# A transformer block on one core: the order of its 512 and 256 column products

## The chip, the core and the metric

The kernel runs on one core of one Trainium2 chip. The metric is the device time of one execution in microseconds (us). Engines are named as in the profile: PE (TensorE matmuls), PEld (its weight loads), DVE (VectorE), ACT (ScalarE), POOL (GpSimd), SP (the DMA queue). L197 is line 197 of the kernel.

## The reference, cut to what matters

One layer of an encoder with 256 tokens, width 2048, float32:

```python
u = rmsnorm(h, g); z = u @ w_in               # 2048 -> [B|C|V|Q|K|V|gate_a|gate_b]
y_a = (b_a * dwconv3(c_a * v_a)) @ w_out_a    # 1024 -> 2048
y_b = windowed_attention(rope(q), rope(k), v, sink) @ w_o_attn
h = h + (sigmoid(gl_a + b) * y_a + sigmoid(gl_b + b) * y_b) @ w_mix_out
up = dwconv3(rmsnorm(h, g2) @ ffn_w_up) + bias          # 2048 -> 2 x 5632
h = h + (silu(up_a) * up_b) @ ffn_w_down                # 5632 -> 2048
return rmsnorm(h, g3)
```

## The kernel before

Nearly all time goes into seven matrix products, each with the 256 tokens as columns. A product is cut into **jobs**: one job makes 128 output rows by adding up `n` blocks of 128 x 128 weights in one PSUM bank (`ps`). `n` is 16 for the input projection, the mixing product and the up-projection, 8 for `w_out_a` and `w_o_attn`, 44 for the down-projection.

Float32 values are split in two: a high part, rounded to the format that PE reads at full rate, and a low part, the rest. The moving operand of a block lies as 512 columns, [high | low] of 256 tokens each (`xs`, `ya_att`, `ms`, `hs`, `actA`, `actC` through the stages). The weights come by DMA as `raw` in chunks of up to eight blocks; ACT makes their high part `whi` (L166), DVE the low part `wlo` (L177). For each block PE then issues two products, called a **pair** here: `whi` times all 512 columns (L197), and `wlo` times the 256 high columns (L198). The products of a job add up in its bank: columns 0 to 255 get high x high and low x high, columns 256 to 511 high x low; an eviction at the job's end adds both halves (`total`: ACT L226, DVE L230).

In a job's last block the order is turned: first the 256 column product, then the 512 column one (L202). The next job begins with its own 512 column product, so that at each job's end two 256s follow each other, and then two 512s. The very last job (`finale`) works with half of the tokens at a time and has an order of its own (L200).

Jobs follow each other in a written list, `groups`. A group of one job goes chunk by chunk of eight blocks. The first group, six jobs, runs block by block across all six; groups made by `outer_first` run three jobs (two in the down-projection) alternately in chunks of four blocks. What else an engine has to do is put between chunks by `run_due` and `step`: a function registered with `at(n, fn)` starts behind the n-th chunk, and a generator goes one step on behind each chunk. Attention's parts are placed so between chunks 29 and 75, and the second norm's sum over the squares (`inv_rms` called by `r2`: PE L240 into `nps`, then ACT, then DVE, a step behind each of three chunks) three chunks behind the end of the mixing product. DVE takes its work in program order, so that a `wlo` behind the norm's last step waits for it.

Of the kernel before, what the change touches and what calls it, by code (L numbers as in the profile page):

```python
# [16 lines left out]
T = 256  # L17
KT = D // P
# [33 lines left out]
def hybrid_block_kernel(ctx: ExitStack, tc: tile.TileContext, head, wide, xT, w_in, w_oa, w_o, w_mix, w_up, w_dn, vec, cst, out):  # L52
    nc = tc.nc
# [18 lines left out]
    def by_half(a):  # L72

        return a.rearrange("p (s h t) -> p h s t", s=2, h=2)
# [3 lines left out]
    def lazy(key, make):  # L78
        if key not in box:
            box[key] = make()  # L80
        return box[key]
# [3 lines left out]
    due, active = [], []  # L85
    now, count = [0], [0]

    def at(n, fn):
        due.append((n, count[0], fn))
        count[0] += 1  # L90
# [4 lines left out]
    def begin(fn, *args):  # L95
        g = fn(*args)
        if hasattr(g, "send") and next(g, 0) != 0:
            active.append(g)
# [6 lines left out]
    def finish():  # L105
        while active:
            step()

    def run_due():
        step()  # L110
        while True:
            ready = sorted(d for d in due if d[0] <= now[0])
            if not ready:
                return
            due.remove(ready[0])
            begin(ready[0][2])

    FETCH, HI, LO = 6, 3, 2
    bank_tags = {}

    def run(groups):

        chunks = []
        for size, jobs, wide in groups:
            n = jobs[0][1]
            if wide:  # L130
                for k in range(n):
                    chunks.append((None, [(job, k) for job in jobs], wide))
                continue
            for k0 in range(0, n, size):
                k1 = min(n, k0 + size)
                for job in jobs:
                    chunks.append((job[0][:, k0:k1, :], [(job, k) for k in range(k0, k1)], None))
        raws, his, los, banks = {}, {}, {}, {}

        def pieces(c):  # L140

            n = len(chunks[c][1])
            return ((0, 2), (2, n)) if c < 3 else ((0, n),)

        def fetch(c):
            w, blocks, pre = chunks[c]
            raw = wpool.tile([P, CH, P], F32, tag="raw", name="raw", bufs=5)
            if pre is not None:
                raws[c] = pre(0, c, raw)
            else:  # L150
                nc.sync.dma_start(raw[:, : len(blocks), :], w)
                raws[c] = lambda a, b, raw=raw: raw[:, a:b, :]


        def high(c):
            _, blocks, pre = chunks[c]
            if pre is not None:
                pre(1, c, None)
            (_, _, _, _, *halves), k0 = blocks[0]
            if halves:  # L160
                last = lazy("last", lambda: cpool.tile([P, FT, P], F32R, tag="B", name="last"))
                his[c] = last[:, k0 : k0 + len(blocks), :]
            else:
                his[c] = wpool.tile([P, CH, P], F32R, tag="whi", name="whi")
            for a, b in pieces(c):
                nc.scalar.copy(his[c][:, a:b, :], raws[c](a, b))  # L166
            if pre is not None:
                pre(2, c, None)

        def low(c):  # L170
            _, blocks, pre = chunks[c]
            if pre is not None:
                pre(3, c, None)
            los[c] = wpool.tile([P, CH, P], F32R, tag="wlo", name="wlo", bufs=3)
            raw = raws.pop(c)
            for a, b in pieces(c):
                nc.vector.tensor_tensor(los[c][:, a:b, :], raw(a, b), his[c][:, a:b, :], op=ALU.subtract)  # L177

        nxt = 0
        for c, (_, blocks, _) in enumerate(chunks):  # L180
            while nxt <= c + FETCH:
                for fn, i in ((fetch, nxt), (high, nxt - FETCH + HI), (low, nxt - FETCH + LO)):
                    if 0 <= i < len(chunks):
                        fn(i)
                nxt += 1
            hi, lo = his.pop(c), los.pop(c)
            ended = []
            for i, (job, k) in enumerate(blocks):
                _, n, rhs, epi, *halves = job
                if k == 0:  # L190
                    tag = bank_tags.get(id(job))
                    pool = aps if tag else lin
                    banks[id(job)] = pool.tile([P, 2 * T], F32, tag=tag or "ps", name="ps")
                ps = banks[id(job)]
                a, last = rhs(k), k == n - 1
                if not last and not (halves and k):
                    nc.tensor.matmul(ps, hi[:, i, :], a, start=k == 0, stop=False)  # L197
                nc.tensor.matmul(ps[:, 0:T], lo[:, i, :], a[:, 0:T], start=False, stop=False)  # L198
                if halves and k:
                    nc.tensor.matmul(by_half(ps)[:, 0], hi[:, i, :], by_half(a)[:, 0], start=False, stop=last)  # L200
                elif last:
                    nc.tensor.matmul(ps, hi[:, i, :], a, start=False, stop=True)  # L202
                if last:
                    ended.append(job)
            now[0] += 1
            run_due()
            for job in ended:
                begin(job[3], banks.pop(id(job)))
        finish()
# [25 lines left out]
    def inv_rms(parts, r, tag="tp"):  # L235

        n = r.shape[-1]
        acc = aps.tile([P, 2 * T], F32, tag=tag, name="nps")[:, 0:n]
        for i, a in enumerate(parts):
            nc.tensor.matmul(acc, ones, a, start=i == 0, stop=i == len(parts) - 1)  # L240
        yield 1
        r0 = spool.tile([P, T], F32, tag="sq", name="r0")[:, 0:n]
        nc.scalar.activation(r0, acc, AF.Ln, bias=eps)
        v = spool.tile([P, T], F32, tag="evt", name="nv")[:, 0:n]
        nc.vector.tensor_scalar(v, acc, EPS, None, op0=ALU.add)
        nc.scalar.activation(r0, r0, AF.Exp, scale=-0.5)
        yield 1

        t = spool.tile([P, T], F32, tag="evs", name="nt")[:, 0:n]
        nc.vector.tensor_tensor(t, r0, r0, op=ALU.mult)  # L250
        nc.vector.scalar_tensor_tensor(t, t, -0.5, v, op0=ALU.mult, op1=ALU.mult)
        nc.vector.scalar_tensor_tensor(r, t, 1.5, r0, op0=ALU.add, op1=ALU.mult)

    def new_r(name):
        rr["r"] = cpool.tile([P, T], F32, tag="r", name=name)
        return rr["r"]
# [190 lines left out]
    def att_turn(t, e):  # L447
        p = probs.pop((t, e))
        tp = aps.tile([P, 2, T], F32, tag="tp", name="ptp")
        for b in range(2):  # L450
            for n in range(2):
                nc.tensor.transpose(tp[:, b, n * P : (n + 1) * P], p[:, n, b * P : (b + 1) * P], ident)  # L452
        yield 1
        pT = p1.tile([P, 2, T], F32, tag="pT", name="pT", bufs=2)
        nc.scalar.copy(pT, tp)
        probs[t, e] = pT

    def att_out(t):
        kv = t // 4
        o = aps.tile([P, 2 * T], F32, tag="av", name="av")  # L460
        pT = [probs.pop((t, e)) for e in range(2)]
        for b in range(2):
            for e in range(2):
                v0 = 128 * kv + 64 * e
                nc.tensor.matmul(  # L465
                    o[64 * e : 64 * e + 64, 0:T], vtok[:, b, v0 : v0 + HD], pT[e][:, b, :], start=b == 0, stop=b == 1
                )
        yield 1
        yield from split(box["B"][:, 8 + t, :], o[:, 0:T])
# [66 lines left out]
    for t in range(8):  # L536
        for n, fn in (
            (0, lambda t=t: att_scores(t, 0)),
            (3, lambda t=t: att_scores(t, 1)),
            (5, lambda t=t: att_turn(t, 0)),  # L540
            (8, lambda t=t: att_turn(t, 1)),
            (10, lambda t=t: att_out(t)),
        ):
            at(29 + 21 * t // 4 + n, fn)

    def start_gates():
        p0.close()
        p1b = p0.enter_context(tc.tile_pool(name="p1b", bufs=1))
        return p1b.tile([P, 2 * KT, T], F32, tag="gates", name="gates")
# [62 lines left out]
    half = {}  # L612

    def r2():
        yield from inv_rms([acc2], new_r("r2"))

    def epi_up(i, which, ps):
        c = i + which * FT
# [115 lines left out]
    jobs = [(w_dn[m], FT, act, lambda ps, m=m: epi_dn(m, ps)) for m in range(KT - 1)]  # L734
    outer_first(jobs + [(w_dn[KT - 1], FT, act, finale, True)], 2)
    run(groups)
    assert not due, due

# [96 lines left out]
```

## Time and profile before

| | us |
|---|---|
| median of 3 runs (1354.37 to 1354.79) | 1354.65 |
| the profiled execution | 1353.56 |
| its span, first to last instruction | 1351.8 |
| PE busy | 1340.5 |
| DVE busy | 971.5 |
| ACT busy | 711.2 |

In the rows of the timeline the first number is an instruction's start from the span's start, the second its time, then the engine, line, operation, what it writes and reads, and how many like it were merged in the row. A matmul's time is its way through the array, longer than the distance to the next one, since they overlap: the distance between starts is what counts.

### The profile page before, as it was taken

To read this page: it belongs to the slowest core of one execution; us is meant where nothing else is said; L and a number is where in the kernel's file an instruction comes from. 1 tells how busy PE (TensorE), PEld (TensorE's weight loads), DVE (VectorE), ACT (ScalarE), POOL (GpSimd) and SP (SyncE) were. 2 spreads that over 40 slices of the span, in tenths; PEclk is the share of its full clock that TensorE was granted. 3 is DMA by queue.
4 is the path that set the end of the run, shared out by engine and by line. 5 is a ranking of instruction groups with operands and counts; after the bars stand their busy time and mean duration, and the time that the engine had idled before them with its cause. 6 is when DMAs were issued, how large, how long until landed. Compare 5 with 4: busy or idle time off the path is not lost.

```text
span 1351.8 us, 20512 instructions
## 1 busy us (share of the span) xinstructions
PE 1340.5 (99%) x7687; PEld 1163.5 (86%) x7687; DVE 971.5 (72%) x1544; ACT 711.2 (53%) x1120; POOL 58.6 (4%) x66
## 2 busy tenths in 40 slices
PE   9999999999999999999999999999999999999997
PEld 8888888888888888888888888888888888888886
DVE  7999887555557887668888888888888865555554
ACT  7656665544445554456555555555555544444441
POOL 0000000000000003420000000000000001001001
PEclk9999999999999999999999999999999999999999
DMA  8776545555555547547555555555555557656663
GB/s 296 231 226 197 188 154 178 184 186 186 187 186 187 187 133 239 186 135 235 186 187 186 187 184 188 186 187 185 186 185 187 169 155 234 187 180 187 187 188 100
DMA packets 75876, 254.23 MB, mean 188 GB/s; under 512 B 8704, under 2 KB 9088, under 8 KB 75776
## 3 DMA queue, kind: packets, MB, share of 16 engines
q1 hardware_dynamic: 75488, 252.52, 58.8%
q8 instruction: 60, 0.98, 0.3%
q10 hardware_dynamic: 288, 0.39, 0.1%
q14 instruction: 40, 0.33, 0.1%
HBM read 248.16 MB, written 2.10 MB: 185 GB/s over the span
## 4 chain that ended last, share of the span: by engine, by line
PE 99%; DVE 0%; DMA 0%; ACT 0%; issue 0%; POOLq 0%; DVEq 0%; ACTq 0%
PE ps L197 60%; PE ps L198 33%; PE ps L202 4%; PE av L465 1%; PE ptp L452 1%; PE ps L200 0%; PE s L423 0%; PE s L422 0%; DMA hd<-in_head_dram 0%; PE more L657 0%; POOLq L830 0%; DVE y L699 0%; DVE r L691 0%; DVE x L664 0%; PE nps L240 0%
## 5 line engine op out<-in xcount | busy, mean ns | idle before, releaser
L177 DVE TENSOR_TENSOR wlo<-raw,whi 128x1024 fp32r<-128x1024 f32 (+2 forms) x494 | 570.8, 1158 | 324.9 <-PE ps L198 230.5
L166 ACT CAST whi<-raw 128x1024 fp32r<-128x1024 f32 (+2 forms) x494 | 488.2, 989 | 349.2 <-PE ps L197 180.0
L197 PE MATMUL ps<-hs,whi 128*128 128x512 f32 x1320 | 470.1, 399 | 0.0
L198 PE MATMUL ps<-hs,wlo 128*128 128x256 f32 x1408 | 381.2, 281 | 0.0
L197 PE MATMUL ps<-xs,whi 128*128 128x512 f32 x1020 | 363.9, 399 | 0.6 <-DVE xs L320 0.6
L197 PEld LDWEIGHTS ps<-hs,whi 128*128 128x128 f32 x1320 | 248.1, 188 | 57.1
L198 PE MATMUL ps<-xs,wlo 128*128 128x256 f32 x1088 | 295.4, 281 | 0.0
L198 PEld LDWEIGHTS ps<-hs,wlo 128*128 128x128 f32 x1408 | 265.8, 189 | 8.9
L197 PEld LDWEIGHTS ps<-xs,whi 128*128 128x128 f32 x1020 | 192.3, 189 | 44.3 <-ACT whi L166 0.9
L198 PEld LDWEIGHTS ps<-xs,wlo 128*128 128x128 f32 x1088 | 206.1, 189 | 5.6 <-DVE wlo L177 0.3
L226 ACT COPY evb<-ps 128x256 f32<-128x256 f32 x188 | 69.7, 372 | 212.2 <-PE ps L202 208.5
L197 PE MATMUL ps<-actC,whi 128*128 128x512 f32 x405 | 143.8, 399 | 0.0
L198 PE MATMUL ps<-actC,wlo 128*128 128x256 f32 x448 | 122.3, 281 | 0.0
L197 PEld LDWEIGHTS ps<-actC,whi 128*128 128x128 f32 x405 | 76.1, 188 | 18.9
L197 PE MATMUL ps<-ms,whi 128*128 128x512 f32 x240 | 85.4, 399 | 0.0
L198 PEld LDWEIGHTS ps<-actC,wlo 128*128 128x128 f32 x448 | 84.7, 189 | 0.8
L197 PE MATMUL ps<-actA,whi 128*128 128x512 f32 x240 | 85.3, 398 | 0.0
L197 PE MATMUL ps<-ya_att,whi 128*128 128x512 f32 x224 | 80.4, 398 | 0.0
L230 DVE TENSOR_TENSOR evt<-ps,evb 128x256 f32<-128x256 f32 x178 | 74.5, 418 | 0.0
L198 PE MATMUL ps<-actA,wlo 128*128 128x256 f32 x256 | 71.1, 281 | 0.0
L198 PE MATMUL ps<-ms,wlo 128*128 128x256 f32 x256 | 69.3, 281 | 0.0
L198 PE MATMUL ps<-ya_att,wlo 128*128 128x256 f32 x256 | 66.6, 281 | 0.0
(149 smaller groups left out, 1159.1 us busy)
## 6 DMA issues: line engine op xcount, KB each, us to landing
raw<-in_w_up_dram SPq DMA_DIRECT2D x170, 512.0 KB, 4.5
raw<-in_w_in_dram SPq DMA_DIRECT2D x124, 512.0 KB, 4.7
raw<-in_w_dn_dram SPq DMA_DIRECT2D x70, 512.0 KB, 4.1
raw<-in_w_mix_dram SPq DMA_DIRECT2D x26, 512.0 KB, 4.8
raw<-in_w_dn_dram SPq DMA_DIRECT2D x36, 256.0 KB, 2.7
raw<-in_w_oa_dram SPq DMA_DIRECT2D x16, 512.0 KB, 3.6
raw<-in_w_o_dram SPq DMA_DIRECT2D x16, 512.0 KB, 3.6
raw<-in_wide_dram SPq DMA_DIRECT2D x15, 512.0 KB, 5.3
```

Of the source, the lines that this page charges most:

```text
L166: nc.scalar.copy(his[c][:, a:b, :], raws[c](a, b))
L177: nc.vector.tensor_tensor(los[c][:, a:b, :], raw(a, b), his[c][:, a:b, :], op=ALU.subtract)
L197: nc.tensor.matmul(ps, hi[:, i, :], a, start=k == 0, stop=False)
L198: nc.tensor.matmul(ps[:, 0:T], lo[:, i, :], a[:, 0:T], start=False, stop=False)
L202: nc.tensor.matmul(ps, hi[:, i, :], a, start=False, stop=True)
L226: nc.scalar.copy(b, ps[:, T : 2 * T])
L230: nc.vector.tensor_tensor(dst, ps[:, 0:T], b, op=ALU.add)
L452: nc.tensor.transpose(tp[:, b, n * P : (n + 1) * P], p[:, n, b * P : (b + 1) * P], ident)
L465: nc.tensor.matmul(o[64 * e : 64 * e + 64, 0:T], vtok[:, b, v0 : v0 + HD], pT[e][:, b, :], start=b == 0, stop=b == 1)
```

## The change

Every pair is now issued as 512 then 256, in a job's last block too; the half-width products of the last job stay as they were. Four chosen pairs are turned (256 then 512): when `turns()` has been called, the next job of 16 blocks that reaches its ninth block (k = 8) fixes the four pairs, 0, 16, 32 and 47 pairs from there. It is called twice: behind chunk 78 (attention's last part starts behind chunk 75), and by `r2` when the second norm's last step is issued. Pairs are counted over all jobs, in the order of issue.

```diff
+    TURNS = (0, 16, 32, 47)
+    pairs = [0]
+    order = {"due": False, "turned": set()}
+
+    def turns():
+        order["due"] = True
...
-                a, last = rhs(k), k == n - 1
-                if not last and not (halves and k):
-                    nc.tensor.matmul(ps, hi[:, i, :], a, start=k == 0, stop=False)
-                nc.tensor.matmul(ps[:, 0:T], lo[:, i, :], a[:, 0:T], start=False, stop=False)
-                if halves and k:
-                    nc.tensor.matmul(by_half(ps)[:, 0], hi[:, i, :], by_half(a)[:, 0], start=False, stop=last)
-                elif last:
-                    nc.tensor.matmul(ps, hi[:, i, :], a, start=False, stop=True)
+                a, last, half = rhs(k), k == n - 1, bool(halves and k)
+                if order["due"] and n == KT and k == KT // 2:
+                    order["due"] = False
+                    order["turned"] = {pairs[0] + d for d in TURNS}
+                turned = half or pairs[0] in order["turned"]
+                pairs[0] += 1
+                both = by_half(ps)[:, 0] if half else ps
+                moving = by_half(a)[:, 0] if half else a
+                products = [
+                    lambda: nc.tensor.matmul(both, hi[:, i, :], moving, start=k == 0, stop=last and turned),
+                    lambda: nc.tensor.matmul(
+                        ps[:, 0:T], lo[:, i, :], a[:, 0:T], start=False, stop=last and not turned
+                    ),
+                ]
+                for product in reversed(products) if turned else products:
+                    product()
...
+    at(78, turns)
...
     def r2():
         yield from inv_rms([acc2], new_r("r2"))
+        turns()
```

PE at a job's end (the first gate job and the start of the second). The numbers behind `ps`, `whi` and `wlo` tell the buffers apart; L197, L198 and L202 of before are L214 and L215 of after. Before:

```order
L197 MATMUL ps_2635<-xs_84,whi_2571 128x512
L198 MATMUL ps_2635<-xs_84,wlo_2605 128x256 x2
L202 MATMUL ps_2635<-xs_84,whi_2571 128x512
L197 MATMUL ps_2690<-xs_84,whi_2603 128x512 [waits Activation_49]
L198 MATMUL ps_2690<-xs_84,wlo_2633 128x256 [waits DVE_49]
```

After:

```order
L214 MATMUL ps_2635<-xs_84,whi_2571 128x512
L215 MATMUL ps_2635<-xs_84,wlo_2605 128x256
L214 MATMUL ps_2690<-xs_84,whi_2603 128x512 [waits Activation_49]
L215 MATMUL ps_2690<-xs_84,wlo_2633 128x256 [waits DVE_49]
L214 MATMUL ps_2690<-xs_84,whi_2603 128x512
```

The two 256s in a row (x2) and the two 512s at the change of bank are gone.

PE in the middle of the second gate job, where a new chunk opens and the first of the turned pairs stands. Before:

```order
L197 MATMUL ps_2690<-xs_84,whi_2603 128x512
L198 MATMUL ps_2690<-xs_84,wlo_2633 128x256
L197 MATMUL ps_2690<-xs_84,whi_2631 128x512 [waits Activation_49]
L198 MATMUL ps_2690<-xs_84,wlo_2663 128x256 [waits DVE_49]
L197 MATMUL ps_2690<-xs_84,whi_2631 128x512
```

After:

```order
L214 MATMUL ps_2690<-xs_84,whi_2603 128x512
L215 MATMUL ps_2690<-xs_84,wlo_2633 128x256
L215 MATMUL ps_2690<-xs_84,wlo_2663 128x256 [waits DVE_49]
L214 MATMUL ps_2690<-xs_84,whi_2631 128x512 [waits Activation_49]
L214 MATMUL ps_2690<-xs_84,whi_2631 128x512
```

The chunk's first 256 stands ahead of its 512 now.

PE behind the second norm, where the three first jobs of the up-projection (`ps_6117`, `ps_6135`, `ps_6154`) alternate: the second turned pair, 24 pairs behind `nps`. Before:

```order
L197 MATMUL ps_6135<-hs_5425,whi_6234 128x512
L198 MATMUL ps_6135<-hs_5425,wlo_6250 128x256 x2
L202 MATMUL ps_6135<-hs_5425,whi_6234 128x512
L197 MATMUL ps_6154<-hs_5425,whi_6248 128x512 [waits Activation_49]
L198 MATMUL ps_6154<-hs_5425,wlo_6264 128x256 [waits DVE_49]
```

After:

```order
L214 MATMUL ps_6135<-hs_5425,whi_6234 128x512
L215 MATMUL ps_6135<-hs_5425,wlo_6250 128x256
L215 MATMUL ps_6154<-hs_5425,wlo_6264 128x256 [waits DVE_49]
L214 MATMUL ps_6154<-hs_5425,whi_6248 128x512 [waits Activation_49]
L214 MATMUL ps_6154<-hs_5425,whi_6248 128x512
```

The turn has moved from the end of the second of these jobs by one pair, to the third job's next chunk. Instructions on DVE, ACT, POOL and SP keep their order, and PE has the same products as before.

More of the change, by code (lines that the diff above doesn't have):

```diff
@@ L194, in run @@
                 ps = banks[id(job)]
-                a, last = rhs(k), k == n - 1
-                if not last and not (halves and k):
-                    nc.tensor.matmul(ps, hi[:, i, :], a, start=k == 0, stop=False)
-                nc.tensor.matmul(ps[:, 0:T], lo[:, i, :], a[:, 0:T], start=False, stop=False)
-                if halves and k:
-                    nc.tensor.matmul(by_half(ps)[:, 0], hi[:, i, :], by_half(a)[:, 0], start=False, stop=last)
-                elif last:
-                    nc.tensor.matmul(ps, hi[:, i, :], a, start=False, stop=True)
+                a, last, half = rhs(k), k == n - 1, bool(halves and k)
[3 more added lines that the diff above has]
+                turned = half or pairs[0] in order["turned"]
+                assert half or not turned or k
+                pairs[0] += 1
[9 more added lines that the diff above has]
+                    product()
                 if last:
```

## The prediction

> **What bounds the kernel now.** I read the page first, then the clock, then the starts of single matmuls, because the page leaves nothing else to read.
>
> ```profile
> PE 1340.5 (99%) x7687; PEld 1163.5 (86%) x7687; DVE 971.5 (72%) x1544; ACT 711.2 (53%) x1120; POOL 58.6 (4%) x66
> PEclk9999999999999999999999999999999999999999
> PE 99%; DVE 0%; DMA 0%; ACT 0%; issue 0%; POOLq 0%; DVEq 0%; ACTq 0%
> core 0: 1351.8 us, clock 0.998
> ```
>
> TensorE is busy for 1340.5 of 1351.8 us, the chain that ended last is PE for 99% of it, and the granted clock is 0.998. So an edit gains or loses what it does to the spacing of matmuls. A "pair" below is one 512-column product on `whi` (L197, or L202 at a job's end) and one 256-column product on `wlo` (L198). Pairs do not all take equal time. Two matmul starts of the first stage, where six jobs share each chunk and nothing is swapped, with the matmuls between left out:
>
> ```profile
> 9.25 0.40 PE L197 MATMUL ps<-xs,whi 128*128 128x512 f32 x1
> ...
> 37.33 0.39 PE L197 MATMUL ps<-xs,whi 128*128 128x512 f32 x1
> ```
>
> 81 pairs lie between them: 28.08 / 81 = 0.3467 us a pair. Now the last products of the jobs (L202), with their count, first and last start by operand:
>
> ```profile
> L202 PE MATMUL ps<-hs,whi x88: 395/400/400, 608.4 to 1091.8; 128*128 128x512 f32 x88
> L202 PE MATMUL ps<-ya_att,whi x32: 396/398/400, 416.0 to 503.4; 128*128 128x512 f32 x32
> L202 PE MATMUL ps<-ms,whi x16: 400/400/400, 517.5 to 593.8; 128*128 128x512 f32 x16
> L202 PE MATMUL ps<-actC,whi x15: 395/396/400, 1121.4 to 1324.8; 128*128 128x512 f32 x15
> ```
>
> Operand `hs` is the up-projection: 8 pairs lie from its first job's end to the third's and 85 x 16 after it, 1368 pairs in 483.4 us, 0.3534 each. `ya_att` has 31 x 8 pairs in 87.4 us, 0.3524; `ms` 8 + 13 x 16 = 216 pairs in 76.3 us, 0.3532; `actC` 4 + 13 x 44 = 576 pairs in 203.4 us, 0.3531. So there are a fast rhythm (0.3467) and a slow one (0.353), 1.9% apart, and all that comes after 244 us is slow. In the slow one a pair of about 0.36 us (below: the long pair) follows every two of 0.35 us, three pairs in 1.06 us.
>
> **What a swap does to the rhythm.** At a job's end the old code already issues the last pair as 256 then 512, the very edit that the new code makes at four chosen pairs. So the trace holds trials of it. Two neighbours, seen at the starts of L197 (a swapped pair shows as L202):
>
> ```profile
> 236.79 0.40 PE L197 MATMUL ps<-xs,whi 128*128 128x512 f32 x1
> ...
> 237.15 0.40 PE L197 MATMUL ps<-xs,whi 128*128 128x512 f32 x1
> ...
> 237.97 0.40 PE L202 MATMUL ps<-xs,whi 128*128 128x512 f32 x1
> 238.21 0.40 PE L197 MATMUL ps<-xs,whi 128*128 128x512 f32 x1
> ...
> 239.26 0.39 PE L197 MATMUL ps<-xs,whi 128*128 128x512 f32 x1
> ...
> 243.07 0.39 PE L197 MATMUL ps<-xs,whi 128*128 128x512 f32 x1
> ...
> 243.54 0.40 PE L202 MATMUL ps<-xs,whi 128*128 128x512 f32 x1
> ...
> 244.46 0.40 PE L197 MATMUL ps<-xs,whi 128*128 128x512 f32 x1
> ...
> 244.82 0.40 PE L197 MATMUL ps<-xs,whi 128*128 128x512 f32 x1
> ```
>
> The long pair starts at 236.79 (0.36 to the next) and is third back from the swapped one (237.97). After that the rhythm is fast: 11 pairs from 239.26 to 243.07, 0.346 each. The next swap (243.54) meets the fast rhythm and ends it: the third pair after it (244.46) is long again. Two more trials:
>
> ```profile
> 429.57 0.40 PE L197 MATMUL ps<-ya_att,whi 128*128 128x512 f32 x1
> 429.81 0.40 PE L198 MATMUL ps<-ya_att,wlo 128*128 128x256 f32 x2
> 430.05 0.40 PE L202 MATMUL ps<-ya_att,whi 128*128 128x512 f32 x1
> ...
> 430.98 0.40 PE L197 MATMUL ps<-ya_att,whi 128*128 128x512 f32 x1
> ...
> 431.34 0.40 PE L197 MATMUL ps<-ya_att,whi 128*128 128x512 f32 x1
> ...
> 432.04 0.40 PE L197 MATMUL ps<-ya_att,whi 128*128 128x512 f32 x1
> ...
> 432.40 0.40 PE L197 MATMUL ps<-ya_att,whi 128*128 128x512 f32 x1
> ...
> 432.87 0.40 PE L202 MATMUL ps<-ya_att,whi 128*128 128x512 f32 x1
> ...
> 434.15 0.40 PE L197 MATMUL ps<-ya_att,whi 128*128 128x512 f32 x1
> ...
> 434.51 0.40 PE L197 MATMUL ps<-ya_att,whi 128*128 128x512 f32 x1
> ```
>
> The pair at 429.57 is long (0.24 from its 512 to its 256, as others have 0.23) and is the one just ahead of the swap (430.05): slow goes on, and the third pair after (430.98) is long. Then 432.04 is long and second back from the swap at 432.87: slow goes on, and the fourth after (434.15) is long. So there are four rules. Long pair one back: slow, long at +3. Two back: slow, long at +4. Three back: fast. Fast before: slow, long at +3.
>
> Without swaps each rhythm keeps itself: the 81 fast pairs above change PSUM bank at every pair and pass chunk after chunk.
>
> **The change part by part.**
>
> *Job ends no longer swapped* (about 200 swaps fall away). The same products remain, so no work goes. A slow stretch stays at 1.06 / 3 = 0.3533 a pair, against 0.3524 to 0.3534 above: nothing, at worst 256 pairs x 0.9 ns = 0.2 us where jobs are 8 long. The eviction now waits for a 256 product instead of a 512 one that ended at the same place; its cover is the next job, 2.8 to 15.5 us of matmuls.
>
> *First four swaps, behind the attention* (pairs 0, 16, 32, 47 from the middle of the second gate job, near 241 us). By the rules, from any of the four states: fast or one back becomes one back at each distance of 16 (+3, +6 ... +15), and at the distance of 15 the long pair is at +12, three back: fast. Two back goes to +4 ... +13, three back at the second swap: fast, then slow at the third, three back at the fourth: fast. Three back is fast, one back at the third, fast after the fourth. All four end fast, near 257 us. It then holds until the sum of squares (`nps`, near 601 us): 440 gate pairs x 6.7 ns = 2.9 us, 256 pairs x 5.7 = 1.5, and 276 pairs of mixing and first up chunks x 6.5 = 1.8. Together 6.2 us.
>
> *Second four swaps, behind the second norm.* Here a wait stands inside the word. Rows of it, and of an earlier one like it:
>
> ```profile
> 601.12 0.59 PE L240 MATMUL nps<-acc,ones 128*128 128x256 f32 x2
> ...
> 606.63 3.27 DVE L177 TENSOR_TENSOR wlo<-raw,whi 128x512 fp32r<-128x512 f32 x4
> ...
> 607.20 0.40 PE L197 MATMUL ps<-hs,whi 128*128 128x512 f32 x1
> ...
> 607.37 0.19 PEld L198 LDWEIGHTS ps<-hs,wlo 128*128 128x128 f32 x1
> ...
> 607.59 0.39 PE L197 MATMUL ps<-hs,whi 128*128 128x512 f32 x1
> ```
>
> ```profile
> 57.27 0.40 PE L197 MATMUL ps<-xs,whi 128*128 128x512 f32 x1
> ...
> 57.51 0.19 PEld L198 LDWEIGHTS ps<-xs,wlo 128*128 128x128 f32 x1 [0.29 <-DVE wlo L177]
> ...
> 57.74 0.39 PE L197 MATMUL ps<-xs,whi 128*128 128x512 f32 x1
> ...
> 58.44 0.40 PE L197 MATMUL ps<-xs,whi 128*128 128x512 f32 x1
> ...
> 58.80 0.40 PE L197 MATMUL ps<-xs,whi 128*128 128x512 f32 x1
> ```
>
> At 607.20 a chunk opens; the load of its `wlo` starts 0.17 us later, not at once, since DVE made it behind the norm's chain (606.63). At 57.27 the same happens, 0.24 us late, released by DVE. There the third pair after the stalled one (58.44) is long. So a stall writes the state anew: long at +3. Counting pairs behind `nps`: the first swap is the 9th, the stalled chunk opens with the 17th, the second swap is the 25th, 8 after the stall. The stall stays, because DVE's chain hangs on `nps`, and a fast PE comes 16 x 6.7 ns = 0.11 us sooner, so 0.17 to 0.28 us late. Long pairs at +3 and +6 of the stall are two back at the second swap: slow, +4 ... +13; three back at the third: fast; the fourth meets the fast rhythm and ends it. The up- and down-projections stay slow: 0, bounded by 13.1 us of gain were they fast (1408 - 76 = 1332 pairs x 6.7 ns = 8.9, and 661 x 6.4 = 4.2), and by 0.1 of loss.
>
> *Before 241 us.* 31 jobs x 16 = 496 pairs run among attention's own matmuls, part fast, part slow. All slow against all fast is 496 x 6.7 ns = 3.3 us. Losing swaps ends some fast stretches less (243.54) and starts others less (237.97); I take 0, ends -1.7 and +1.7.
>
> *Sum.* -6.2 + 0 + 0 on a span of 1351.8 gives 1345.6. The profiled execution took 1353.56, 1.76 beside its span, so 1347.4; the median of the runs is 1.09 above it: 1348.4 us, 1346.7 to 1350.1.
>
> [...]
>
> **Rivals.**
> - *Both words work, 1335.3 us.* The stall's rule rests on one other trial (57.51); if a longer wait leaves a long pair elsewhere, or none, the second word ends fast as the first does: 1348.4 - 13.1. For it: three of the four states at the second swap would do. Against: both stalls go on alike, the next 512 coming 0.22 or 0.23 us after the late load (607.37 to 607.59, 57.51 to 57.74).
> - *The swaps do not set the rhythm, 1354.7 us.* One disturbed pair in the 972 after the first word makes the rest slow, and no fast stretch after 38 us is longer than a job in this trace. If it breaks soon each time, or spacing follows columns alone, the gain is under 1 us. Against: 81 fast pairs in a row among eviction and loads.
> - *Denser matmuls lower the granted clock, slower.* Place: from 257 us on, 1090 us bound by PE. Each 1% costs 10.9 us; beyond 0.6% it eats the 6.2, beyond 0.8% the kernel is slower by over 0.2%: at 1% 1359. Against: 0.998 for the whole span, fast first stage included. [...]
>
> **How the numbers follow.** Fast to the norm, slow behind it: 0.48, the forecast. Both words: 0.33. Only the second word or a rhythm broken halfway, 1339 to 1345: 0.05. No effect: 0.10. Clock: 0.04. About 0.2% (2.7 us) is what a measurement of this kernel can tell from no change; the first three are faster, 0.86. The range takes the first two with their 1.7 us: 1333.6 to 1350.1; the forecast's own is 1346.7 to 1350.1.
>
> **What the profile after would show.** Right: starts of 512 products 0.3467 apart from 260 to 594 us; `nps` near 595 us; one late `wlo` load some 6 us behind it; then three pairs in 1.06 us to the end, but for 15 fast pairs between the third and fourth swap. Both words: fast pairs there too, a span near 1332. Wrong: a stall or slow triple between 260 and 594 us, no late load behind `nps`, or a clock under 0.99.

## The result

The changed kernel takes 1334.68 us (median of 4 runs, 1334.36 to 1335.65) against 1354.51 us (1353.88 to 1354.79) for the kernel before (4 runs): a ratio of 0.9855, interval 0.9838 to 0.9873. That is 20 us less, not the 6 us of the forecast: the time of the rival "both words work" (1335.3). A "word" is here, as in the prediction, one set of four turned pairs.

The page and the clock of the changed kernel, whose profiled execution took 1335.65 us:

```profile
PE 1322.7 (99%) x7687; PEld 1161.9 (87%) x7687; DVE 968.7 (73%) x1544; ACT 712.9 (53%) x1120; POOL 70.0 (5%) x66
core 0: 1333.9 us, clock 0.998
```

Between the two profiled executions the span is 17.9 us shorter, and PE is busy 17.8 us less with the same 7687 matmuls at the same clock. So the gain lies in the spacing of the products. (The medians are 19.8 us apart: the profiled execution of before, 1353.56, was faster than its four runs above, that of after, 1335.65, the slowest of its four.) To place the gain, the last matmul of attention (`av`) of before and of after, and after's sum of squares (`nps`); before's `nps`, 601.12, stands in the prediction.

```profile
L465 PE MATMUL av<-pT,vtok x64: 379/379/431, 108.3 to 229.3; 128*64 128x256 f32 x64
```

```profile
L483 PE MATMUL av<-pT,vtok x64: 379/379/431, 109.6 to 230.9; 128*64 128x256 f32 x64
...
596.41 0.59 PE L258 MATMUL nps<-acc,ones 128*128 128x256 f32 x2
```

- Up to the last `av`: 229.3 before, 230.9 after, +1.6 us.
- From there to `nps`: 371.8 and 365.5, -6.3 us.
- From `nps` to the end of the span: 750.7 and 737.5, -13.2 us.

The products of four operands in the trace of after (matmul durations: lowest, median, highest in ns; then the first and the last start):

```profile
L214 PE MATMUL ps<-hs,whi x1408: 391/391/582, 589.5 to 1078.0; 128*128 128x512 f32 x176
...
L214 PE MATMUL ps<-actC,whi x420: 391/391/391, 1089.5 to 1306.8; 128*128 128x512 f32 x140
...
L214 PE MATMUL ps<-ya_att,whi x256: 391/391/391, 412.0 to 500.4; 128*128 128x512 f32 x128
...
L214 PE MATMUL ps<-ms,whi x256: 391/391/391, 500.7 to 589.1; 128*128 128x512 f32 x128
```

`ms`: 88.4 us over 255 distances, 0.3467 a pair. `hs`: 488.5 over 1407, 0.3472, the second word included. Both are the fast rhythm, where before had 0.3532 and 0.3534.

The two places on which the forecast turned. First, the fourth turned pair behind the attention (its 512 opens the row x2 at 259.20) in the timeline of after:

```profile
258.73 0.40 PE L214 MATMUL ps<-xs,whi 128*128 128x512 f32 x1
...
259.20 0.63 PE L214 MATMUL ps<-xs,whi 128*128 128x512 f32 x2
...
260.14 0.39 PE L214 MATMUL ps<-xs,whi 128*128 128x512 f32 x1
...
260.49 0.39 PE L214 MATMUL ps<-xs,whi 128*128 128x512 f32 x1
...
260.84 0.39 PE L214 MATMUL ps<-xs,whi 128*128 128x512 f32 x1
```

From 260.14 on the starts are 0.35 apart with no 0.36 among them, and so it is at all 969 pairs up to `nps`. Second, the late `wlo` load between the second word's first and second turned pair:

```profile
602.44 0.40 PE L214 MATMUL ps<-hs,whi 128*128 128x512 f32 x1
...
602.66 0.19 PEld L215 LDWEIGHTS ps<-hs,wlo 128*128 128x128 f32 x1
...
603.24 0.39 PE L214 MATMUL ps<-hs,whi 128*128 128x512 f32 x1
...
603.58 0.39 PE L214 MATMUL ps<-hs,whi 128*128 128x512 f32 x1
...
603.93 0.39 PE L214 MATMUL ps<-hs,whi 128*128 128x512 f32 x1
```

The load is 0.22 us late, as foreseen. But the rhythm behind it is fast: the pair at +3 (603.58, counted from the stalled pair 602.44) takes 0.35 us, where the forecast had the long one. The second turned pair then finds the fast state instead of "two back", and the second word ends fast. Below, "+1", "+2" and "+3" are short for what a late load leaves: slow, with the first long pair that many pairs behind the stalled one.

### The profile page after: what moved, and what is told of

Its sections match the earlier page's. It is cut to its first block, busy times and chain, and to the rows that moved or that the text cites. A ratio compares the mean times of both kernels' runs of the same rounds, so it can differ in the third digit from the quotient of the medians.

```text
span 1333.9 us, 20498 instructions
## 1 busy us (share of the span) xinstructions
PE 1322.7 (99%) x7687; PEld 1161.9 (87%) x7687; DVE 968.7 (73%) x1544; ACT 712.9 (53%) x1120; POOL 70.0 (5%) x66
## 4 chain that ended last, share of the span: by engine, by line
PE 99%; DVE 0%; DMA 0%; ACT 0%; issue 0%; POOLq 0%; DVEq 0%; ACTq 0%
PE ps L214 63%; PE ps L215 33%; PE av L483 1%; PE ptp L470 1%; PE s L440 0%; PE s L441 0%; DMA hd<-in_head_dram 0%; PE more L677 0%; POOLq L850 0%; DVE y L719 0%; DVE r L711 0%; DVE x L684 0%; PE nps L258 0%; ACT ln L701 0%; PE nps L699 0%
## 5 line engine op out<-in xcount | busy, mean ns | idle before, releaser
L214 PE MATMUL ps<-hs,whi 128*128 128x512 f32 x1408 | 488.4, 391 | 0.0
L215 PE MATMUL ps<-hs,wlo 128*128 128x256 f32 x1408 | 393.7, 280 | 0.0
L214 PE MATMUL ps<-xs,whi 128*128 128x512 f32 x1088 | 384.1, 397 | 0.6 <-DVE xs L338 0.6
L214 PEld LDWEIGHTS ps<-hs,whi 128*128 128x128 f32 x1408 | 263.1, 187 | 57.6
L215 PE MATMUL ps<-xs,wlo 128*128 128x256 f32 x1088 | 304.8, 281 | 0.0
L215 PEld LDWEIGHTS ps<-hs,wlo 128*128 128x128 f32 x1408 | 266.1, 189 | 0.5
L214 PEld LDWEIGHTS ps<-xs,whi 128*128 128x128 f32 x1088 | 204.8, 188 | 48.1 <-ACT whi L175 1.2
L215 PEld LDWEIGHTS ps<-xs,wlo 128*128 128x128 f32 x1088 | 206.4, 190 | 0.4
L214 PE MATMUL ps<-actC,whi 128*128 128x512 f32 x420 | 146.2, 391 | 0.0
L215 PE MATMUL ps<-actC,wlo 128*128 128x256 f32 x448 | 124.4, 280 | 0.0
L214 PEld LDWEIGHTS ps<-actC,whi 128*128 128x128 f32 x420 | 78.5, 187 | 17.2
L214 PE MATMUL ps<-ya_att,whi 128*128 128x512 f32 x256 | 88.8, 391 | 0.0
L214 PE MATMUL ps<-ms,whi 128*128 128x512 f32 x256 | 88.8, 391 | 0.0
L215 PEld LDWEIGHTS ps<-actC,wlo 128*128 128x128 f32 x448 | 84.8, 189 | 0.0
L214 PE MATMUL ps<-actA,whi 128*128 128x512 f32 x240 | 83.8, 391 | 0.0
L215 PE MATMUL ps<-ya_att,wlo 128*128 128x256 f32 x256 | 71.7, 280 | 0.0
L215 PE MATMUL ps<-ms,wlo 128*128 128x256 f32 x256 | 71.7, 280 | 0.0
L215 PE MATMUL ps<-actA,wlo 128*128 128x256 f32 x256 | 70.9, 280 | 0.0
```

The source lines that it names most:

```text
L214: lambda: nc.tensor.matmul(both, hi[:, i, :], moving, start=k == 0, stop=last and turned),
L215: lambda: nc.tensor.matmul(ps[:, 0:T], lo[:, i, :], a[:, 0:T], start=False, stop=last and not turned),
```

## The experiments

The theory after the result: the four rules on turned pairs hold, and what a late `wlo` load leaves behind is not fixed. Its rivals: the late load always leaves the fast rhythm here; or the turned pairs do not matter, and it is enough that the turns at the job ends are gone.

**One word, the other, none, and one pair elsewhere.** The first leaves out the second word, the second the first word, the third both; the fourth moves the last turned pair of each word by one.

```diff
 e1_first_word:   in r2
-        turns()
 e2_second_word:
-    at(78, turns)
 e3_no_swaps: both lines out
 e4_last_at_48:
-    TURNS = (0, 16, 32, 47)
+    TURNS = (0, 16, 32, 48)
```

> Only the four swaps behind the attention stay; the second call of turns() is left out. If the swaps set a rhythm that carries on (rules theory), PE is fast (0.3467 us a pair) from 257 us to the norm, and behind it the late wlo load decides: fast on gives 1334.8 us, slow gives 1348. If such a late load always leaves the long pair three pairs on (the prediction's step), it is slow there: 1348. If pure alternation is fast by itself and the swaps do nothing, 1334.7 with no slow stretch anywhere.

> Only the four swaps behind the second norm stay. Rules theory: slow (three pairs in 1.06 us) from the attention to the norm; the wlo load comes 0.17 us late as in the kernel before, leaves the long pair at +3, two back at the second swap, so the word ends slow: 1354.4; if the late load leaves anything else, the word ends fast: 1341. If the swaps do nothing and alternation alone is fast: 1334.7.

> Pure alternation, no swap at all but in the last half-width job. Rules theory: slow to the norm; the wlo load 0.17 us late leaves slow as before: 1354.4 (1341 if it leaves fast). If alternation alone is fast: 1334.7.

> The last of each four swaps is one pair later (0, 16, 32, 48). Rules theory: at the fourth swap the long pair is one back (+3 ... +15) instead of three back, so each word ends slow whatever came before: 1354.5, with up to 32 fast pairs inside a word. If four swaps near there are what matters and not their distance, or alternation alone is fast: 1334.7.

Before took 1353.1 to 1354.9 us in 21 executions beside these.

- First word only: eight executions at two times. Three took 1334.3 to 1335.8, five 1347.4 to 1348.8; the ratio over all is 0.9913 (0.9873 to 0.9954). The profiled one took 1348.3.
- Second word only: 1340.83 and 1341.66.
- No words: again two times, three at 1340.5 to 1342.2 and five at 1354.3 to 1354.9; ratio 0.9976 (0.9939 to 1.0012). The profiled one took 1340.54.
- Last turned pair at 48: all eight at 1352.7 to 1354.5, ratio 1.0 (0.9989 to 1.0011).

The late load in the first-word kernel, profiled at 1348.3 us, and its products on `hs`:

```profile
601.72 0.39 PE L214 MATMUL ps<-hs,whi 128*128 128x512 f32 x1
...
601.98 0.19 PEld L215 LDWEIGHTS ps<-hs,wlo 128*128 128x128 f32 x1 [0.19 <-DVE wlo L186]
...
602.91 0.40 PE L214 MATMUL ps<-hs,whi 128*128 128x512 f32 x1
...
603.27 0.40 PE L214 MATMUL ps<-hs,whi 128*128 128x512 f32 x1
```

```profile
L214 PE MATMUL ps<-hs,whi x1408: 390/398/582, 588.8 to 1086.3; 128*128 128x512 f32 x176
```

The load comes 0.26 us late, the pair at +3 (602.91) is long, 0.36 us, and nothing turns a pair afterwards: 497.5 / 1407 = 0.3536 a pair, slow to the end. This is the forecast's own case. Now the kernel without words, profiled at 1340.54 us:

```profile
607.60 0.40 PE L214 MATMUL ps<-hs,whi 128*128 128x512 f32 x1
...
607.77 0.19 PEld L215 LDWEIGHTS ps<-hs,wlo 128*128 128x128 f32 x1
...
608.69 0.39 PE L214 MATMUL ps<-hs,whi 128*128 128x512 f32 x1
...
609.04 0.39 PE L214 MATMUL ps<-hs,whi 128*128 128x512 f32 x1
```

```profile
L214 PE MATMUL ps<-hs,whi x1408: 391/391/582, 594.4 to 1082.9; 128*128 128x512 f32 x176
```

Slow up to here, then a load 0.17 us late, as late as in the trace of before, and 488.5 / 1407 = 0.3472 a pair from there on: the late load alone made it fast. So a late load can leave either rhythm, and "always fast" falls with the first-word kernel. "No turns are enough" falls with the fourth kernel: it too has no turns at job ends, and moving one pair of each word by one place brings it back to the time of before. By the rules it must: at distances of 16 a pattern that starts one back stays one back, and whatever the late load leaves, the last turned pair finds one back or the fast rhythm, both of which end slow. Its products show the slow rhythm:

```profile
L214 PE MATMUL ps<-hs,whi x1408: 387/398/582, 593.2 to 1090.7; 128*128 128x512 f32 x176
...
L214 PE MATMUL ps<-ms,whi x256: 395/398/403, 502.7 to 592.8; 128*128 128x512 f32 x128
```

`ms` takes 90.1 / 255 = 0.3533, `hs` 497.5 / 1407 = 0.3536: slow from the first word on, and the second does not help.

**How often, and a word behind the late load.** By the rules only "long at +3" makes the second word end slow; fast, +1 and +2 all end fast. So with the word where the change has it, some executions must come out 13 us longer. Called eight chunks later, the word stands wholly behind the late load, and must end fast whatever that leaves.

```diff
 e5_word_behind_stall, b2_word_behind, b3_word_behind:   in r2
-        turns()
+        later(8, turns)
 a1_after_again, b2_after_again, b3_after_again: the changed kernel itself
 a2_second_again: e2_second_word itself
```

> The second word starts eight chunks later, so that all its swaps lie behind the late wlo load. By the four rules it ends fast from every state: all executions 1334.7 to 1335.0 (a few tenths more where some 60 pairs behind the load are slow). If the rules do not hold for the states that a late load leaves: some near 1348.

> The changed kernel itself, for more executions. With one word alone or none, 10 of 16 executions went on slow behind the late load and 6 fast. Theory coin: the late load leaves fast or long at +3 by chance here too, and +3 is two back at the second swap and ends slow, so about 5 of 8 executions take 1348 and 3 of 8 take 1334.7 (four of four fast so far would be luck of 1 in 50). Theory place: with the first swap 8 pairs ahead of the late load its outcome is always one from which the word ends fast: all 1334.7.

> Only the four swaps behind the second norm, again. Both executions so far took 1341 (fast behind the norm). Theory coin: 5 of 8 executions 1354.4, the rest 1341. Theory place: all 1341.

> The second word wholly behind the late load, more executions: all 1334.0 to 1336, whatever the load leaves.

> The second word wholly behind the late load, once more: none of these executions near 1348, all 1334.0 to 1336.

> The changed kernel, more executions: eight so far were all fast. Of 84 late loads made on purpose 19 (23%) left the long pair at +3, the one state from which this word ends slow by the four rules. If the late load here is drawn from the same lot, 2 of each 8 to 9 executions take 1348; if this place never gives +3, none.

> The changed kernel once more: at a chance of 23% some execution of these and the other four near 1348, at none all 1334.7.

| kernel | executions | near the lower time | near the higher time |
|---|---|---|---|
| changed kernel, first result included | 18 | 17: 1333.2 to 1335.7 | 1: 1347.14 |
| word behind the late load | 12 | 12: 1334.0 to 1335.9 | 0 |
| second word only, both times | 12 | 8: 1340.5 to 1341.9 | 4: 1352.5 to 1354.8 |

So two expectations missed: a late load that leaves the slow rhythm in 5 of 8 executions does not fit the changed kernel, and a place that always gives the better time is refuted by 1347.14 and by the second word alone.

The ratios to before are 0.9853 (0.9839 to 0.9868), 0.9868 (0.9841 to 0.9895) and 0.9853 (0.9838 to 0.9867) for the changed kernel, 0.9859 (0.9843 to 0.9875), 0.9855 (0.9842 to 0.9868) and 0.9858 (0.9845 to 0.9871) with the word behind: no difference in the usual time. The second word alone gave 0.9943 (0.9914 to 0.9973) over ten executions of both kinds.

The second word alone was profiled at 1354.08 us, and there the forecast's chain is seen step by step. The late load, then the second, third and fourth turned pair (the rows x2):

```profile
607.68 0.40 PE L214 MATMUL ps<-hs,whi 128*128 128x512 f32 x1
...
608.77 0.40 PE L214 MATMUL ps<-hs,whi 128*128 128x512 f32 x1
...
609.13 0.40 PE L214 MATMUL ps<-hs,whi 128*128 128x512 f32 x1
...
609.83 0.40 PE L214 MATMUL ps<-hs,whi 128*128 128x512 f32 x1
...
610.66 0.63 PE L214 MATMUL ps<-hs,whi 128*128 128x512 f32 x2
...
616.30 0.64 PE L214 MATMUL ps<-hs,whi 128*128 128x512 f32 x2
...
617.59 0.39 PE L214 MATMUL ps<-hs,whi 128*128 128x512 f32 x1
...
620.71 0.39 PE L214 MATMUL ps<-hs,whi 128*128 128x512 f32 x1
...
621.52 0.62 PE L214 MATMUL ps<-hs,whi 128*128 128x512 f32 x2
...
622.44 0.40 PE L214 MATMUL ps<-hs,whi 128*128 128x512 f32 x1
...
622.80 0.40 PE L214 MATMUL ps<-hs,whi 128*128 128x512 f32 x1
```

Long at +3 (608.77) and +6 (609.83), which is two back from the turned pair at 610.66: slow. Behind the next (616.30) the pattern is fast: nine pairs from 617.59 to 620.71, 0.347 each. The last (621.52) meets the fast rhythm and ends it: 622.44, the third after it, is long. The same program was also profiled in an execution of 1340.83 us. There the load at 607.68 is 0.17 us late too, but the pair at +3 takes 0.35 us:

```profile
607.68 0.40 PE L214 MATMUL ps<-hs,whi 128*128 128x512 f32 x1
...
608.77 0.39 PE L214 MATMUL ps<-hs,whi 128*128 128x512 f32 x1
...
609.12 0.39 PE L214 MATMUL ps<-hs,whi 128*128 128x512 f32 x1
```

One program, the same rules, another outcome of the late load, and 13 us between the two.

With the word behind, a late load that did leave "long at +3" no longer costs anything. The third kernel of the three:

```profile
601.65 0.39 PE L214 MATMUL ps<-hs,whi 128*128 128x512 f32 x1
...
602.84 0.40 PE L214 MATMUL ps<-hs,whi 128*128 128x512 f32 x1
...
603.20 0.40 PE L214 MATMUL ps<-hs,whi 128*128 128x512 f32 x1
```

```profile
L214 PE MATMUL ps<-hs,whi x1408: 390/391/582, 588.7 to 1077.5; 128*128 128x512 f32 x176
```

The pair at 602.84 (+3) is long, yet the median matmul on `hs` is 391 ns, the fast rhythm's, and the execution took 1335.16 us. The second of the three shows the same, with 1335.3 us.

**Many late loads.** To see whether lateness sets the outcome, a kernel without words gives DVE work of growing width ahead of each up-projection job from the fourth on, and an addition of zero to the job's first `wlo` block, so that its load comes late.

```diff
+            if j is not None:
...
+                w = 4 + 8 * (j // 2 % 44) + 4 * (j % 2)
+                for n in [T] * (2 if j % 2 else 1) + [w]:
+                    nc.vector.tensor_tensor(ct[:, 0:n], ct[:, 0:n], ct[:, 0:n], op=ALU.subtract)
+                nc.vector.tensor_tensor(los[c][:, 0, :], ct[:, 512 : 512 + P], los[c][:, 0, :], op=ALU.add)
```

> No swaps; ahead of each up-projection job from the fourth on DVE does some 0.4 to 1.1 us of extra work (subtractions in a dead table, and adding zero to the first block of that job's wlo) whose width grows by 8 columns every second job, so that the first wlo load of up to 85 jobs comes late by different times. Theory chance: outcomes fast and slow mix with no order in the lateness, about 3 in 8 fast. Theory phase: the outcome follows the lateness with a period of a few ns to some 10 ns, a band of fast, a band of slow. Prediction's rule (always long at +3): all slow. The time is longer by the stalls, about 85 x 0.1 to 0.4 us.

It took 1372.95 us, and its trace holds 84 loads that are 0.05 to 0.75 us late, the norm's own among them: 48 left the fast rhythm, 19 "+3", 13 "+2", 1 "+1", and 3 a third pattern (described at the end). So "always long at +3" is refuted, and fast is commoner than the 3 in 8 expected. To the 10 ns that the rows show, lateness does not sort them: of 12 loads late by 210 to 240 ns 7 left fast, 3 "+3"; of 26 late by 350 to 450 ns 15 fast, 6 "+3", 5 "+2". Two that agree to 10 ns up to the first pair behind, both out of the fast rhythm (L222 and L223 are the 512 and 256 products of this kernel):

```profile
732.90 0.39 PE L222 MATMUL ps<-hs,whi 128*128 128x512 f32 x1
...
733.12 0.19 PEld L223 LDWEIGHTS ps<-hs,wlo 128*128 128x128 f32 x1
...
734.04 0.39 PE L222 MATMUL ps<-hs,whi 128*128 128x512 f32 x1
...
734.39 0.39 PE L222 MATMUL ps<-hs,whi 128*128 128x512 f32 x1
```

```profile
778.82 0.39 PE L222 MATMUL ps<-hs,whi 128*128 128x512 f32 x1
...
779.04 0.19 PEld L223 LDWEIGHTS ps<-hs,wlo 128*128 128x128 f32 x1
...
779.96 0.40 PE L222 MATMUL ps<-hs,whi 128*128 128x512 f32 x1
...
780.32 0.40 PE L222 MATMUL ps<-hs,whi 128*128 128x512 f32 x1
```

Both loads are 0.22 us late. The pair at +3 takes 0.35 us in the first case, 0.36 in the second, and so the two go on. For whoever writes the program the outcome is a draw so far. But the other theory of the expectation, that of a phase, is not refuted. The trace holds starts to the nanosecond. Take the 49 loads that came out of the fast rhythm, divide each one's lateness (from the start of its pair to the start of the load) by 6.667 ns and keep the remainder:

| remainder | loads | left |
|---|---|---|
| 1.3 to 3.0 ns | 15 | 11 "+3", 4 fast |
| under 0.7 or over 5.9 ns | 19 | 9 "+2", 9 fast, 1 third pattern |
| between these | 15 | 13 fast, 1 "+3" (the load at 779.04 above), 1 third pattern |

The period was picked after the outcomes were seen, as the best of all between 2.5 and 60 ns; with the same outcomes dealt out by chance, 200 times, none fitted as well. The rhythm before may count too: of the 18 loads whose stalled pair stood right behind a long one, 14 left the fast rhythm. No run was built to test either.

What stays open: what the phase is and whether it decides alone; the four profiles of the changed kernel have loads 221 to 230 ns late, so that it would differ between executions. And whether the place matters: 19 of 84 late loads left "+3" here, and 4 of 12 executions of the second-word kernel took the higher time, but only 1 of 18 of the changed kernel. These counts are too small to tell rarer from luck. (The first four kernels ran on one chip, the other runs of this section on another.)

## Why the prediction was wrong

- *Two rhythms, no work added or lost:* right. PE's busy time fell with the span at equal counts, and away from turned pairs and late loads the stretches from 260 us on have 0.3467 or 0.3533 us a pair in each of the twelve traces without turns at job ends and without extra work.
- *The four rules on a turned pair:* right at all 76 turned pairs of the eleven traces that have words, all four cases among them (30 "three back", 23 "fast before", 12 "one back", 11 "two back"). That moving the last pair to 48 loses the whole gain is what they demand. They are not the whole truth: in the trace of before, three job ends ahead of 206 us met the fast rhythm and left the third pattern.
- *First word, -6.2 us up to `nps`:* right, -6.3 between the last `av` and `nps`.
- *Before 241 us, 0 within 1.7:* +1.6, inside the bound. It is not a cost of the change that can be counted on: the last `av` lies between 228.3 and 230.9 in the same twelve traces (228.7 to 230.9 in the four of the changed kernel alone), and at 229.3 in before.
- *"So a stall writes the state anew: long at +3":* this is the step that failed, and with it the term of 0 for the up- and down-projections, which measured -13.2 (the working's own bound for it was 13.1). The rule stood on one trial, and that one (57.27) had a turned pair right ahead of it, at 57.03. In the other late load that the prediction quoted, before's at 607.20, a turned job end at 608.41 comes three pairs later, so that the trace could not show what the load had left. The measured outcomes are fast, +1, +2 or +3 (and, in 3 of 84, the third pattern, for which the rules say nothing), and by the rules three of these four let the second word end fast. The forecast's case does occur: its chain stands in the profile of the second word alone, and the execution of the changed kernel at 1347.14 has its time. But that came once in 18, where I had given it 0.48.
- *Rivals:* "both words work" happened, at its price. "The swaps do not set the rhythm" is refuted by the kernel with the last pair at 48. That rival also allowed for spacing that follows columns alone; the runs disagree: the kernel without words, with one order of equal products up to its last job, took 1340.5 or 1354.9 us. "Denser matmuls lower the clock" is refuted by 0.998 in the spans of both.

The rows of the two turned pairs of before, at 57.03 and 608.41:

```profile
57.03 0.40 PE L202 MATMUL ps<-xs,whi 128*128 128x512 f32 x1
...
608.41 0.40 PE L202 MATMUL ps<-hs,whi 128*128 128x512 f32 x1
```

Why before never drew the better time: behind the late load its job ends turn a pair every 4, then every 16, then every 44 pairs. By the rules each state comes to "one back" within a few turns at distances of 16, stays there, and changes between one and two back at 44: slow, whatever the load left. This is worked out from the rules; it fits the 0.3534 a pair in the trace of before.

## What to carry to other kernels

Where PE is busy 99% of the span, compare start-to-start distances of equal matmuls by stretch before looking for waits: here 1.5% of the time lay in a rhythm that busy shares do not show. A short run of turned pairs that ends in the good rhythm from every state is, by the four rules, worth more than one that does so from the usual state; place it behind the last wait that can disturb it (here 0 of 12 executions took the higher time so, against 1 of 18 with the wait inside the word, too few to tell apart). Which turns do that has to be found anew for other products: the four rules here are read from pairs of 512 and 256 columns alone. And a rule that rests on one trial in a trace deserves a rival with even odds, and a program several executions: one program can have two times, 13 us apart.

## What the runs showed of the hardware

- One program at one granted clock (0.998) took 1340.83 or 1354.08 us in two profiled executions, by what one weight load, 0.17 us late in both, left behind for over 700 us. Two other programs took 1334.3 or 1348.3 us and 1340.5 or 1354.9 us; each of these was profiled in one execution only.
- Two late loads with rows equal to 10 ns up to the next pair go on in different rhythms (733.12 and 779.04). To the nanosecond, what 49 late loads left goes in part with their lateness modulo 6.67 ns.
- Where a turned pair meets the rhythm decides how it goes on, at 76 of 76 turned pairs: three back fast, otherwise slow.
- Products overlap: in before's rows a 512 column one stands with 0.40 us and the next starts 0.23 us behind it (224.31, 224.54), a 256 column one with 0.28 us and the next starts 0.12 behind it (224.54, 224.66).
- The rounded format (`fp32r` in the rows of DVE and ACT) is the faster of the two that PE reads here. From the start of a `wlo` product (256 columns of it, 600.65 in before) to that of the second product behind it (601.00) 0.35 us pass; from the start of `nps` (256 columns in float32, 601.12), 0.66 (601.78); in both a 512 column product stands between. Whether it is PE's full rate no run shows.
- A third pattern, in 3 of the 84 late loads: pairs of 0.343 and 0.350 us by turns, whose mean, 0.3467, is the fast rhythm's.
